# Up product of a hybrid encoder block: twelve of its tiles regrouped from pairs into threes, and the weight forms of every pair split 1024 columns at a time

## The chip, the cores and the metric

One core of one Trainium2 chip runs the whole kernel. The metric is the device time of one execution in microseconds (us), shown as the median of several runs. The profile and its trace are of one execution of the same program; times in it count from the start of its span.

## The reference

One layer of an encoder trunk over x of 512 tokens by 1024 features, all in float32:

```python
h  = rmsnorm(x, g_pre_mix)
q, k, v, g, u, sv, a_ret, a_sgu = split(h @ w_in)
merged = sigmoid(a_ret) * retention(q, k, v, g) @ w_ret_o + sigmoid(a_sgu) * sgu(u, sv) @ w_sgu_o
x  = x + rmsnorm(merged @ w_out, g_post_mix)
h2 = rmsnorm(x, g_pre_ffn)
hid = conv3(h2 @ w_up) + conv_b          # 1024 -> 2 * 2816, width-3 convolution over the tokens, per channel
a, b = split(hid)
x  = x + rmsnorm((gelu(a) * b) @ w_down, g_post_ffn)
```

The change is about `h2 @ w_up` (the up product) and about the way in which the weights of some products are made ready.

## The kernel before, in words

**Precision.** Every float32 operand of a matmul is split into a high part, which TensorE's fp32r format holds, and the rest: ScalarE copies the operand into the high tile, and VectorE subtracts that from the operand (`split`, lines 117 to 119). A product of two such operands is three matmuls, high by high, high by low and low by high (`mm3`, lines 299 to 302).

**Weights.** All weights come as tiles of 128 by 1024 from one array `wall`. A list of units, `units` (lines 126 to 159), gives the order in which they are used. `w_get` hands out the next unit and, ahead of use, has further units loaded and split so long as they fit in a look-ahead of nine slots; the slots (`w4`, nine of 128 by 1088) hold the finished high and low tiles, and four raw tiles (`raw`) hold what a DMA of SyncE's queue brings. A block unit (`w_block`) takes two slots: one for a high tile of 1024 columns, one for the low one.

**Blocks and pairs.** The up product makes 22 tiles of the hidden layer. A tile has two output blocks of 128 channels by 512 tokens, one for `a` and one for `b`. There are two ways to make a tile. Plain: two calls of `f_block`, each 8 x 3 matmuls with 512 moving columns, into one PSUM bank. In seven products (class `Pair`): the two blocks together by a Strassen-Winograd scheme, seven products of 4 x 3 matmuls with 256 moving columns, into three PSUM banks, with sums and differences of the activations made once beforehand (`h2_forms`). The products are spread over `part1` (four), `part2` (one) and `part3` (two). `part1` copies the first product out of its bank before the fourth adds to the same bank, `part2` reads bank 2 before `part3` adds to it, and the results end in two SBUF tiles `c` from a pool of six (`tmp`).

**Forms.** A pair needs seven weight operands of 512 columns: B11, B21, T1 to T4 and B22, where T1 to T4 are sums of the four quarters of the raw weights. In the kernel before, each is a unit of its own (`w_form`, lines 194 to 215), with one copy on ScalarE and one subtraction on VectorE of 512 columns, and one slot that holds the high and the low part. The four sums are additions of 512 columns on VectorE; for the gate weights two of them (T2, T4) are on GpSimd. Pairs are also used for the u product (4 pairs) and for the two gates (8 pairs), whose order is the hand-written list `MIDDLE`.

**Order in the up product.** Tiles 0 to 3 are plain. Tiles 4 to 19 go in couples (`COUPLES`): one tile as a pair, one plain. A couple runs `part1`, the first block of the plain tile, `part2`, half of the second block, `part3`, and the other half. Tiles 20 and 21 are plain. After its products each tile goes through `tile_done` (line 1309): for each of its blocks a scaled copy on ScalarE and two multiply-adds on VectorE (`conv`), then a gelu on ScalarE and a product on VectorE (`gated`). After certain tiles (7, 9, 11, 13, 17, and 19 to 21) `down_forms` prepares activations for the down product: four additions and one split on VectorE, more work on ScalarE and GpSimd's DMAs. The down product follows, with weight units "q" and "t" (`w_down`) that need three additions and two splits for each step.

**Order of the engines.** Instructions are traced in program order, and a planner in the framework puts them on each engine's queue by priority, readiness and its own estimate of costs; tiles of a pool are handed out as earlier ones come free. An engine then runs its queue in the order that was fixed.

Of the kernel before, what the change touches and what calls it, by code (L numbers as in the profile page):

```python
# [13 lines left out]
ALU = mybir.AluOpType  # L14

P = 128
# [27 lines left out]
COUPLES = [(i, i + 1) for i in range(4, 20, 2)]  # L44
# [8 lines left out]
def tile_block(ctx: ExitStack, tc, xT, x, wall, par, cs, wsp, bsp, gpost, gffn, out):  # L53
# [71 lines left out]
    FORMS = ("B11", "B21", "T1", "T2", "T3", "T4", "B22")  # L125
    units = []
    i = 0
    while i < NW:
# [6 lines left out]
        elif i == U0:  # L135
            us, gs = ([[(f, k + n * m) for f in FORMS] for n in range(KD // 2)] for k, m in ((U0, 2), (GATE0, 4)))
            ws = [("blk", GATE0 + 4 * (n // 2) + 2 + n % 2) for n in range(KD)]
            for what, n in MIDDLE:
                units += {"W": lambda: ws[n : n + 1], "U1": lambda: us[n][:4], "U2": lambda: us[n][4:],
                          "G1": lambda: gs[n][:4], "G2": lambda: gs[n][4:]}.get(what, list)()  # L140
            i = GATE0 + 2 * KD
        elif GATE0 <= i < GATE1:
            units += pair[:4] + [("blk", i + 2)] + pair[4:] + [("blk", i + 3)]
            i += 4
        elif i == UP0 + 2 * COUPLES[0][0]:
            for a, b in COUPLES:
                pair = [(f, UP0 + 2 * a) for f in FORMS]
                units += pair[:4] + [("blk", UP0 + 2 * b)] + pair[4:] + [("blk", UP0 + 2 * b + 1)]
            i = UP0 + 2 * COUPLES[-1][1] + 2
# [44 lines left out]
    def w_form(form, i):  # L194

        if form == "B11":
            a, b = raw_tile(), raw_tile()
            nc.sync.dma_start(a, wall[i])
            nc.sync.dma_start(b, wall[i + 1])
            w_raw["B11"], w_raw["B12"] = a[:, :S], a[:, S:]  # L200
            w_raw["B22"], w_raw["B21"] = b[:, :S], b[:, S:]
        elif form == "T1":
            t = raw_tile()
            w_raw["T1"], w_raw["T2"], w_raw["T3"], w_raw["T4"] = t[:, :S], t[:, S:], w_raw["B12"], t[:, S:]
            nc.vector.tensor_add(w_raw["T1"], w_raw["B11"], w_raw["B12"])
            nc.vector.tensor_add(w_raw["T3"], w_raw["B12"], w_raw["B22"])
            eng = nc.vector if i < GATE0 or i >= UP0 else nc.gpsimd
            eng.tensor_tensor(out=w_raw["T2"], in0=w_raw["T1"], in1=w_raw["B22"], op=ALU.add)
        elif form == "T4":
            eng = nc.vector if i < GATE0 or i >= UP0 else nc.gpsimd  # L210
            eng.tensor_tensor(out=w_raw["T4"], in0=w_raw["T2"], in1=w_raw["B21"], op=ALU.add)
        w = slot("wf", 0, 1088)
        lo, hi = w[:, AT_64 : AT_64 + S], w[:, S + AT_192 : 2 * S + AT_192]
        split(hi, lo, w_raw[form])
        return hi, lo
# [65 lines left out]
    def w_size(u):  # L281
        return 2 if u[0] in ("blk", "q", "t") or u[0][0] == "s" else 1
# [626 lines left out]
    class Pair:  # L909
# [9 lines left out]
        def product(self, b, act, first, w=None):  # L919
            wh, wl = w or w_get()  # L920
# [21 lines left out]
        def part1(self):  # L942
# [3 lines left out]
            def second():  # L946
                o = self.product(1, self.x(4, T0), True)
                self.sum = v.tensor_add(two(c0[:, T0]), o, two(c0[:, T0])).ins

            o = self.product(0, self.x(0, T0), True)  # L950
            copy(two(c0[:, T0]), o)
            second()
            self.product(2, self.s("S1"), True)
            o = self.product(0, self.s("S2"), False)
# [4 lines left out]
        def part2(self):  # L959
            c0, c1 = self.t  # L960
            o = self.product(0, self.s("S3"), False)
            copy(two(c1[:, T1]), o)
            v.tensor_sub(two(c1[:, T1]), self.two(self.b[2][:, T0]), two(c1[:, T1]))
            self.w = w_get(), w_get()
# [344 lines left out]
    def tile_done(i, o):  # L1309
        gated(*(conv(t, 2 * i + s_) for s_, t in enumerate(o)))  # L1310
        if i < COUPLES[-1][1]:
# [18 lines left out]
    couples = dict(COUPLES)  # L1330
    i = 0
    while i < NF:
        if i in couples:
            p = Pair(None, lambda: tmp("c"), (h2h, h2l, h2forms))
            p.part1()
            o = [f_block(h2h, h2l, KD)]
            p.part2()
            o.append(f_block(h2h, h2l, KD, p.part3))
            tile_done(i, p.t)
            tile_done(i + 1, o)  # L1340
            i += 2
# [237 lines left out]
def _two(a):  # L1579
# [3 lines left out]
        np.concatenate([b[:, 0, :, 0], b[:, 1, :, 0]], -1), np.concatenate([b[:, 1, :, 1], b[:, 0, :, 1]], -1),  # L1583
# [3 lines left out]
def _up(a):  # L1587

    for i, _ in COUPLES:
# [89 lines left out]
```

## Time and profile before

| what | value |
|---|---|
| median of 3 runs | 783.18 us (782.7 to 783.85) |
| span of the profiled execution | 782.6 us (no other time is given for it) |
| busy TensorE / weight load / VectorE / ScalarE / GpSimd | 774.5 / 720.7 / 639.5 / 485.2 / 103.5 us |
| granted TensorE clock, mean | 0.997 |
| matmul records | 5139 |
| HBM read / written | 91.34 MB / 4.19 MB |

Busy time is the union of an engine's instructions. Matmuls and VectorE's instructions overlap their neighbours at the ends, so the time that one more of them costs is read from start to start, not from its own length. In the text PE is TensorE, PEld its weight load, DVE VectorE, ACT ScalarE, POOL GpSimd and SP SyncE; L926 is line 926 of the kernel before.

### The profile page before, as it was taken

To read this page: it belongs to the slowest core of one execution; us is meant where nothing else is said; L and a number is where in the kernel's file an instruction comes from. 1 tells how busy PE (TensorE), PEld (TensorE's weight loads), DVE (VectorE), ACT (ScalarE), POOL (GpSimd) and SP (SyncE) were. 2 spreads that over 40 slices of the span, in tenths; PEclk is the share of its full clock that TensorE was granted. 3 is DMA by queue.
4 is the path that set the end of the run, shared out by engine and by line. 5 is a ranking of instruction groups with operands and counts; after the bars stand their busy time and mean duration, and the time that the engine had idled before them with its cause. 6 is when DMAs were issued, how large, how long until landed. Compare 5 with 4: busy or idle time off the path is not lost.

```text
span 782.6 us, 13472 instructions
## 1 busy us (share of the span) xinstructions
PE 774.5 (99%) x5139; PEld 720.7 (92%) x5139; DVE 639.5 (82%) x1093; ACT 485.2 (62%) x878; POOL 103.5 (13%) x132
## 2 busy tenths in 40 slices
PE   9999999999999999999999999999999999999996
PEld 8888998998999999999998998999999998999996
DVE  6567987789789988877765679989999889886987
ACT  7555568688466766644454686657777568644542
POOL 0040001130021102033211200001111012200001
PEclk9999999999999999999999999999999999999998
DMA  8783224453223233233459120435555375733344
GB/s 288 271 246 102 81 82 162 108 122 108 81 91 126 82 122 121 83 110 106 138 171 337 54 81 28 124 107 141 142 148 149 108 199 111 171 114 107 109 162 162
DMA packets 35889, 104.80 MB, mean 134 GB/s; under 512 B 4400, under 2 KB 6320, under 8 KB 35824
## 3 DMA queue, kind: packets, MB, share of 16 engines
q1 hardware_dynamic: 27936, 87.81, 34.0%
q0 software_dynamic: 7024, 14.95, 9.0%
q10 hardware_dynamic: 864, 1.18, 0.4%
q8 instruction: 40, 0.66, 0.4%
q14 instruction: 25, 0.20, 0.1%
HBM read 91.34 MB, written 4.19 MB: 122 GB/s over the span
## 4 chain that ended last, share of the span: by engine, by line
PE 92%; DVE 3%; DMA 3%; issue 1%; ACT 0%; POOLq 0%; DVEq 0%; POOL 0%; ACTq 0%
PE ps L926 24%; PE ps L300 12%; PE ps L302 12%; PE ps L301 12%; PE ps L1372 7%; PE ps L755 5%; PE ps L634 4%; PE ps L636 4%; PE ps L635 4%; DMA raw<-wall 3%; PE ps L1109 2%; PE ps L1108 2%; PE ps L1107 2%; DVE dl L119 1%; PE ps L997 1%
## 5 line engine op out<-in xcount | busy, mean ns | idle before, releaser
L119 DVE TENSOR_TENSOR wl<-raw,wh 128x1024 fp32r<-128x1024 f32 (+1 forms) x84 | 96.0, 1152 | 54.3 <-issue 19.1
L100 ACT ACTIVATE wf<-raw 128x512 fp32r<-128x512 f32 x140 | 85.6, 625 | 67.3 <-PE ps L301 19.4
L926 PE MATMUL ps<-sh,wf 128*128 128x256 f32 x640 | 117.4, 276 | 0.1
L119 DVE TENSOR_TENSOR wf<-raw,wf 128x512 fp32r<-128x512 f32 x140 | 107.0, 774 | 9.2 <-ACT wf L100 8.6
L926 PEld LDWEIGHTS ps<-sh,wf 128*128 128x128 f32 x640 | 101.9, 192 | 1.1 <-ACT sig L100 0.5
L100 ACT ACTIVATE wh<-raw 128x1024 fp32r<-128x1024 f32 (+2 forms) x88 | 84.8, 977 | 28.5 <-DMA raw<-wall 14.0
L300 PE MATMUL ps<-h2h,wh 128*128 128x512 f32 (+1 forms) x256 | 90.6, 354 | 0.0
L301 PE MATMUL ps<-h2l,wh 128*128 128x512 f32 (+1 forms) x256 | 90.4, 353 | 0.0
L302 PE MATMUL ps<-h2h,wl 128*128 128x512 f32 (+1 forms) x256 | 90.4, 353 | 0.0
L926 PE MATMUL ps<-sl,wf 128*128 128x256 f32 x320 | 88.0, 275 | 0.0
L926 PEld LDWEIGHTS ps<-sl,wf 128*128 128x128 f32 x320 | 61.4, 192 | 0.4
L1372 PE MATMUL ps<-dh,fh 128*128 128x256 f32 x216 | 59.6, 276 | 0.3 <-DVE yy L1409 0.3
L1372 PE MATMUL ps<-dl,fh 128*128 128x256 f32 x216 | 59.5, 275 | 0.0
L1372 PE MATMUL ps<-dh,fl 128*128 128x256 f32 x216 | 59.4, 275 | 0.0
L100 ACT ACTIVATE dh<-raw 128x768 fp32r<-128x768 f32 (+1 forms) x36 | 33.6, 950 | 33.8 <-DVE raw L231 15.2
L302 PEld LDWEIGHTS ps<-h2h,wl 128*128 128x128 f32 x256 | 48.6, 190 | 5.1
L301 PEld LDWEIGHTS ps<-h2l,wh 128*128 128x128 f32 x256 | 48.6, 190 | 4.5
L300 PEld LDWEIGHTS ps<-h2h,wh 128*128 128x128 f32 x256 | 48.6, 190 | 4.5
L926 PE MATMUL ps<-xh,wf 128*128 128x256 f32 x288 | 52.2, 275 | 0.0
L636 PE MATMUL ps<-wh,xl 128*128 128x512 f32 x128 | 48.5, 379 | 0.0
L635 PE MATMUL ps<-wl,xh 128*128 128x512 f32 x128 | 48.5, 379 | 0.0
L634 PE MATMUL ps<-wh,xh 128*128 128x512 f32 x128 | 48.5, 380 | 0.0
(343 smaller groups left out, 2171.6 us busy)
## 6 DMA issues: line engine op xcount, KB each, us to landing
raw<-wall SPq DMA_DIRECT2D x144, 512.0 KB, 3.7
x<-x SPq DMA_DIRECT2D x24, 256.0 KB, 6.0
fl<-gp POOLq DMA_DIRECT2D x12, 256.0 KB, 3.8
swap<-qkraw POOLq DMA_DIRECT2D x16, 128.0 KB, 4.8
x<-x POOLq DMA_DIRECT2D x8, 256.0 KB, 2.3
fl<-fs POOLq DMA_DIRECT2D x8, 256.0 KB, 4.3
xT<-xT SPq DMA_DIRECT2D x7, 256.0 KB, 5.0
xT<-xT POOLq DMA_DIRECT2D x4, 256.0 KB, 4.1
```

Source lines behind the costliest of these rows:

```text
L100: return nc.scalar.activation(out=o, in_=i, func=AF.Copy)
L119: low[0] = nc.vector.tensor_sub(lo, src, as32(hi)).ins
L300: nc.tensor.matmul(o, ah, bh, start=start, stop=False, skip_group_check=skip)
L301: nc.tensor.matmul(o, ah, bl, start=False, stop=False, skip_group_check=skip)
L302: pe_last[0] = nc.tensor.matmul(o, al, bh, start=False, stop=stop, skip_group_check=skip).ins
L634: nc.tensor.matmul(acc[t], xh[k][:, c], turns(wh[:, f]), start=k == 0, stop=False)
L635: nc.tensor.matmul(acc[t], xh[k][:, c], turns(wl[:, f]), start=False, stop=False)
L636: part_end[0] = nc.tensor.matmul(acc[t], xl[k][:, c], turns(wh[:, f]), start=False, stop=k == KD - 1)
L755: nc.tensor.matmul(bank[t], a_[:, c], turns(w_[:, f]), start=first and k == i == 0, stop=last and k == 3 and i == 2, skip_group_check=True,)
L926: self.last = nc.tensor.matmul(o, w_[:, c], a_, start=first and k == n == 0, stop=k == 3 and n == 2, skip_group_check=True,)
L1107: nc.tensor.matmul(o, ah, turns(bh), start=k == 0, stop=False)
L1372: nc.tensor.matmul(o, a_[:, c], turns(w_[:, f]), start=j == t == i == 0, stop=j == DP - 1 and i == 2 and n not in (M2, M3, M4), skip_group ...
```

## The change

`COUPLES` becomes `GROUPS`: (4, 5) and (6, 7) stay couples, and tiles 8 to 19 go in four groups of three, (8, 9, 10) to (17, 18, 19). In a three the first and the last tile go in seven products and the middle one is plain, so that ten tiles are made in seven products where there were eight. A three runs: `part1` of the first tile, the first half of a block of the middle tile, `part2`, the other half of that block, `part3`, `tile_done` of the first tile; then the same with the last tile and the middle tile's second block, with `tile_done` of the middle tile ahead of the last `part3`.

The seven forms become four units: B1 (B11 and B21 in one raw tile), T12 and T34 of 1024 columns and two slots each, and B22 of 512 columns and one slot. A copy and a subtraction of 1024 columns take the place of two of 512. The sums are the same four additions; T34 is now written over the raw tile of B1. This holds for all pairs, those of the u product and of the gates too. The host's layout of the raw weights changes to suit.

```diff
-COUPLES = [(i, i + 1) for i in range(4, 20, 2)]
+GROUPS = [(4, 5), (6, 7)] + [(i, i + 1, i + 2) for i in range(8, 20, 3)]
...
-    FORMS = ("B11", "B21", "T1", "T2", "T3", "T4", "B22")
+    FORMS = ("B1", "T12", "T34", "B22")
...
+            for a, b, *c in GROUPS:
                 pair = [(f, UP0 + 2 * a) for f in FORMS]
+                b = [("blk", UP0 + 2 * b + n) for n in range(2)]
+                if c:
+                    last = [(f, UP0 + 2 * c[0]) for f in FORMS]
+                    units += pair[:2] + b[:1] + pair[2:] + last[:2] + b[1:] + last[2:]
+                else:
+                    units += pair[:2] + b[:1] + pair[2:] + b[1:]
...
+        eng = nc.vector if i < GATE0 or i >= UP0 else nc.gpsimd
+        if form == "B1":
+            a, b = w_raw["a"], w_raw["b"] = raw_tile(), raw_tile()
             nc.sync.dma_start(a, wall[i])
             nc.sync.dma_start(b, wall[i + 1])
+            w_raw["B22"], w_raw["B12"] = b[:, :S], b[:, S:]
+            raw = a
+        elif form == "T12":
+            raw = w_raw["t"] = raw_tile()
+            nc.vector.tensor_add(raw[:, :S], w_raw["a"][:, :S], w_raw["B12"])
+            eng.tensor_tensor(out=raw[:, S:], in0=raw[:, :S], in1=w_raw["B22"], op=ALU.add)
+        elif form == "T34":
+            raw = w_raw["a"]
+            nc.vector.tensor_add(raw[:, :S], w_raw["B12"], w_raw["B22"])
+            eng.tensor_tensor(out=raw[:, S:], in0=w_raw["t"][:, S:], in1=raw[:, S:], op=ALU.add)
+        if form == "B22":
+            w = slot("wf", 0, 1088)
+            lo, hi = w[:, AT_64 : AT_64 + S], w[:, S + AT_192 : 2 * S + AT_192]
+            raw = w_raw["B22"]
+        else:
+            hi, lo = slot("wf", AT_192), slot("wf", AT_64)
+        split(hi, lo, raw)
...
-        return 2 if u[0] in ("blk", "q", "t") or u[0][0] == "s" else 1
+        return 1 if u[0] == "B22" else 2
...
+                o = [f_block(h2h, h2l, KD, p.part2)]
+                p.part3()
+                tile_done(i, p.t)
+                p = Pair(None, lambda: tmp("c"), (h2h, h2l, h2forms))
+                p.part1()
+                o.append(f_block(h2h, h2l, KD, p.part2))
+                tile_done(i + 1, o)
+                p.part3()
+                tile_done(i + 2, p.t)
```

`Pair` takes its operands through a new method `halves`, which gets one unit of 1024 columns and hands out its two halves.

84 lines of the change are left out of this document (35 added, 49 removed).

## The prediction

> **What bounds the kernel now.** I read the page's busy times and the shares of its chain first.
>
> ```profile
> span 782.6 us, 13472 instructions
> PE 774.5 (99%) x5139; PEld 720.7 (92%) x5139; DVE 639.5 (82%) x1093; ACT 485.2 (62%) x878; POOL 103.5 (13%) x132
> PE 92%; DVE 3%; DMA 3%; issue 1%; ACT 0%; POOLq 0%; DVEq 0%; POOL 0%; ACTq 0%
> ```
>
> TensorE holds 92% of the chain, so a matmul less is a gain only while the others keep up. Whether they do is read from the stages: two windows of the middle part, the eight couples of the up product, the last two plain tiles, and the entry into the down product (columns: PE, PEld, DVE, ACT, POOL, clock, DMA share, GB/s).
>
> ```profile
> 210.00:320.00 110.00, 110.00 (x849) 105.95 (x848) 96.91 (x163) 73.11 (x125) 17.88 (x13) 1.00 0.32 101
> 320.00:401.00 81.00, 80.91 (x554) 75.68 (x553) 63.65 (x94) 41.10 (x69) 17.71 (x12) 1.00 0.42 137
> ...
> 490.28:510.02 19.74, 19.74 (x135) 18.45 (x134) 19.11 (x31) 13.52 (x25) 1.83 (x2) 1.00 0.50 146
> 510.02:529.76 19.74, 19.74 (x135) 18.45 (x134) 16.89 (x27) 11.18 (x20) 0.00 (x0) 1.00 0.35 107
> 529.76:549.50 19.74, 19.74 (x135) 18.45 (x134) 18.16 (x31) 14.22 (x28) 3.50 (x4) 1.00 0.54 140
> 549.50:569.24 19.74, 19.74 (x135) 18.45 (x134) 18.15 (x31) 14.18 (x28) 3.50 (x4) 1.00 0.53 141
> 569.24:588.98 19.74, 19.74 (x135) 18.45 (x134) 18.48 (x32) 14.71 (x27) 2.59 (x3) 1.00 0.56 147
> 588.98:608.72 19.74, 19.74 (x135) 18.45 (x134) 18.49 (x32) 14.72 (x27) 2.56 (x3) 1.00 0.58 147
> 608.72:628.46 19.74, 19.74 (x135) 18.45 (x134) 16.90 (x27) 11.29 (x20) 0.00 (x0) 1.00 0.32 108
> 628.46:648.20 19.74, 19.74 (x134) 18.45 (x133) 16.26 (x29) 13.58 (x25) 3.03 (x4) 1.00 0.66 175
> 648.20:668.76 20.56, 20.56 (x98) 17.98 (x96) 19.47 (x35) 16.40 (x26) 4.65 (x6) 1.00 0.61 128
> 668.76:685.00 16.24, 16.24 (x146) 16.16 (x144) 14.56 (x24) 11.88 (x19) 3.71 (x5) 1.00 0.68 175
> ```
>
> Each couple takes the same 19.74 us and PE is full. But DVE is busy for 16.3 to 19.1 us of them: in this stage it is a second bound just behind the first. ACT (at most 14.72) and the DMAs (share at most 0.66) are not.
>
> **The matmuls.** The chain of waits in order of time gives their pace in one couple (start, length).
>
> ```profile
> 490.28 5.36 PE ps L926 x48
> 495.64 0.22 PE ps L300
> ...
> 500.82 1.34 PE ps L926 x12
> 502.16 0.22 PE ps L300
> ...
> 504.75 2.68 PE ps L926 x24
> ...
> 510.02 5.36 PE ps L926 x48
> ...
> 540.30 1.34 PE ps L926 x12
> ```
>
> A product of 12 matmuls of 256 columns takes 1.34 us (5.36 / 48 = 0.1117 each); a block of 24 matmuls of 512 columns goes from 495.64 to 500.82, 5.18 us. A tile in seven products takes 5.36 + 1.34 + 2.68 = 9.38 us, a plain one 2 x 5.18 = 10.36, so one more tile in seven products saves 0.98, and two save 1.96 us. The Trainium skill, page TensorE: Matmul & The Clock Gate, section Back-to-back issue gap, gives an isolated matmul on a warm clock N / 2.4 + 2.5 ns and says that this under-counts where N is small. By it the gap for 256 columns would be 109.2 ns, the pair 9.17 us and the saving an estimated 2.4 us instead of 1.96; the trace has 111.7 ns, so the measurement decides for 1.96.
>
> **VectorE's work.** Its timeline gives costs from start to start.
>
> ```profile
> 528.13 0.68 DVE L119 TENSOR_TENSOR wf<-raw,wf 128x512 fp32r<-128x512 f32 x1
> ...
> 630.12 0.75 DVE L1254 SCALAR_TENSOR_TENSOR cv<-c,part,cv 128x511 f32<-128x511 f32 x1
> 630.78 0.74 DVE L1254 SCALAR_TENSOR_TENSOR cv<-ps,part,cv 128x511 f32<-128x511 f32 x1
> 631.44 0.68 DVE L1263 TENSOR_TENSOR gp<-cv,cv 128x512 f32<-128x512 f32 x1
> 632.04 0.74 DVE L1250 SCALAR_TENSOR_TENSOR cv<-ps,part,cv 128x511 f32<-128x511 f32 x1
> ...
> 635.22 0.42 DVE L1289 TENSOR_TENSOR fs<-gp,gp 128x256 f32<-128x256 f32 x1
> 635.56 1.22 DVE L119 TENSOR_TENSOR wl<-raw,wh 128x1024 fp32r<-128x1024 f32 x1
> 636.69 0.42 DVE L1290 TENSOR_TENSOR fs<-fs,gp 128x256 f32<-128x256 f32 x1
> ```
>
> A multiply-add costs 0.66, an operation of 512 columns 0.60, of 1024 1.13, of 256 0.34 us. A pair's tile before: seven subtractions 4.20, four sums 2.40, three evacuations of 256 columns 1.02, four multiply-adds 2.64, the gating 0.60, together 10.86. With the merged forms the subtractions are 3 x 1.13 + 0.60 = 3.99 and the tile 10.65, a saving of 0.21. A plain tile is 2.26 + 2.64 + 0.60 = 5.50. The sum for a couple before, 16.36, stands against 16.89 busy in the couple that has no `down_forms`, a factor of 1.03; `down_forms` adds 1.3 to 1.6 (18.16 and 18.49 less 16.9), say 1.4.
>
> A three costs DVE (2 x 10.65 + 5.50) x 1.03 = 27.6 us, and PE 2 x 9.38 + 10.36 = 29.12. With `down_forms` after tiles 9; 11 and 13; none; and 17, the four threes need 29.0, 30.4, 27.6 and 29.0 of 29.12: 116.0 for PE's 116.5. DVE's spare time, 1 to 3 us in each couple before, is gone. The first three also inherits the evacuation of both tiles of couple (6, 7), 6.5 us where a three leaves about 4.5, so a backlog of 2.0 + 1.3 = 3.3 us builds up by the end of tiles 11 to 13.
>
> What covers it: weights are ready long ahead. The T3 form whose subtraction starts at 528.13 is used at 540.30, so weights may be 10 us late. What does not wait as long is the emptying of PSUM banks. The rows of one `part2`, from the chain and from the timelines of ACT and DVE:
>
> ```profile
> 560.04 1.34 PE ps L926 x12
> ...
> 562.25 0.37 ACT L100 ACTIVATE c<-ps 128x256 f32<-128x256 f32 x1
> ...
> 562.99 0.42 DVE L963 TENSOR_TENSOR c<-ps,c 128x256 f32<-128x256 f32 x1
> ...
> 565.40 1.23 DVE L119 TENSOR_TENSOR wl<-raw,wh 128x1024 fp32r<-128x1024 f32 x1 [1.40 <-issue]
> ...
> 569.54 0.75 DVE L1250 SCALAR_TENSOR_TENSOR cv<-ps,part,cv 128x511 f32<-128x511 f32 x1
> ```
>
> The subtraction that empties bank 2 ends at 563.33; S4's product needs the bank at 560.04 + 1.34 + 2.59 + 1.34 = 565.31, 2.0 us later. In a three `part2` comes half a block (2.59 us) earlier, while one tile less (3.24 us) is evacuated ahead of it, which leaves 2.6 us against a backlog of up to 3.3. Two smaller deadlines join it: the next `part1` writes a `c` tile that the last tile's or the middle tile's evacuation must have freed, and ACT's copies of banks stand in its queue behind a T12 that now waits for both of its sums. PE's waits in the threes thus lie between 0 (the planner puts evacuations first) and 3.3 us (the whole backlog). I take 1.0, nearer to the excess of 0.7 than to the whole.
>
> **The entry into the down product.** Here the lead is gone already before:
>
> ```profile
> 683.77 1.22 DVE L119 TENSOR_TENSOR dl<-raw,dh 128x1024 fp32r<-128x1024 f32 x1
> 684.92 0.68 DVE L226 TENSOR_TENSOR raw<-raw 128x512 f32<-128x512 f32 x1
> ...
> 684.84 0.28 PE L1372 MATMUL ps<-dh,fh 128*128 128x256 f32 x1
> 685.05 0.38 PE L1372 MATMUL ps<-dl,fh 128*128 128x256 f32 x1
> ```
>
> The split ends at about 684.92; PE's two starts stand 0.21 apart where 0.11 is its pace, so PE waits 0.1 us for it. If PE comes 1.96 us earlier, DVE must too. The cost lies between 0 (DVE's chain hangs on PE's end of tile 19 and moves along) and 1.96 (DVE comes no earlier). The last couple's 16.26 shows 3.5 us of idle DVE, since the weights that follow are four plain blocks, and most of the backlog can go there; I take 0.4.
>
> **Other parts, at nothing.** The 12 pairs of the middle stages save DVE 0.21 us each; PE was full there (110.00 of 110, 80.91 of 81), so no gain. Their T12 waits for GpSimd's T2 before either half can be split:
>
> ```profile
> L208 POOL TENSOR_TENSOR raw<-raw,raw 128x512 f32<-128x512 f32 x8 | 13.3, 1660 | 90.6 <-DMA raw<-wall 74.2 <-DVE raw L205 16.4
> ```
>
> 1.66 us, covered by a lead like the 10 us above; without cover, two sums in each of eight pairs would cost 26 us. DMAs: a three loads eight raw tiles of 0.52 MB in 29.12 us, 144 GB/s, where a couple loads five in 19.74, 133 GB/s; rows of 175 GB/s stand beside a full PE. The new turn of the raw tiles lets the next B1 load only after T34's split, still some 10 us ahead of use. Coarser units leave the slots the same: pair and block fill nine, as before.
>
> **Sum.** -1.96 + 1.0 + 0.4 = -0.56 us. The profiled span of 782.6 is 0.6 below the median of 783.18, and I apply the difference to the median: 782.6 us. What this measurement can tell from no change is about 0.2%, 1.57 us, so this forecast is no change.
>
> **Rivals.** *PE stays fed* (0.33): the planner lets evacuations pass, DVE's chain into the down product moves along, and the waits stay under 0.38 us: 783.18 - 1.96 = 781.2. For it: no PE gap in eight couples at up to 19.11 us of DVE. Against: 116.0 of 116.5. *VectorE's queue becomes the bound* (0.24), the other side: at 565.40 DVE idles 1.40 us for a slot while a finished bank, read only at 569.54, could have been worked on. Where such idling stays in the threes, there is no slack to take it. Half of 1.40 in each of the eight halves is 5.6 us: 783.18 - 1.96 + 5.6 = 786.8; it decides from 0.44 us a half, 3.5 in all. The Trainium skill, same page, section on the array's architecture (16x 32x32), says that ACT's and DVE's queues are strict FIFO; by that rule no ready work passes a waiting head, and the trace's 1.40 us agrees.
>
> **Chances.** No change 0.43 (waits from 0.38 to 3.5 us), faster 0.33, slower 0.24. The range, 781.0 to 786.0, reaches from the fed case to the middle of the slower one and leaves out about 0.2; the likeliest case alone is 781.6 to 784.7.
>
> **What would show it.** Right: 72 more matmuls, threes of 29.1 us in the chain plus 0.1 to 0.5 each in front of an S2, S4 or T4 product, released by ACT or DVE; DVE over 28 us busy in the threes with tiles 9, 11, 13 and 17; a PE gap at the third or fourth step of the down product. Wrong: PE gaps at `wf` tiles (weights late), gaps in the gates' stage behind POOL, or DVE with several us to spare in the threes.

## The result: 0.7% slower

The changed kernel takes 788.70 us (median of 6, 788.00 to 791.97) against 783.23 us (median of 6, 782.70 to 783.85): a ratio of 1.0072 (95% interval 1.0059 to 1.0086), 5.5 us slower where 0.6 us faster was forecast.

The spans must be brought to one footing first. Wherever a run of these two kernels is listed with its span, the run takes 1.7 to 1.9 us longer (788.33 for the profiled 786.6 here; 783.32 for 781.6 of the kernel before, in a later comparison). By that, an estimate, the profiled execution of before, with its span of 782.6, was one of about 784.4, above the six runs counted here (single later runs go beyond it). This is most of the reason why the spans differ by 4.0 us and the medians by 5.5. It also means that the stage lengths of before, below, are together about 1 us too long, and it is not known in which stage.

The page of the changed kernel (span, busy time by engine):

```profile
span 786.6 us, 13545 instructions
PE 773.9 (98%) x5211; PEld 721.9 (92%) x5211; DVE 642.7 (82%) x1051; ACT 482.9 (61%) x830; POOL 105.6 (13%) x132
```

There are 72 matmuls more, as the change intends, and PE is busy 0.6 us less in a span that is 4.0 us longer: PE waits. The windows by stage say where. Before the change (middle part from the first product of a pair, w_out with the transposes and plain tiles, up product from the first couple, down product; columns as in the prediction):

```profile
210.20:403.02 192.82, 192.73 (x1409) 183.21 (x1408) 162.53 (x258) 114.73 (x194) 36.87 (x26) 1.00 0.36 115
403.02:490.12 87.10, 87.10 (x514) 79.28 (x512) 63.24 (x120) 56.53 (x140) 11.34 (x19) 1.00 0.34 122
490.12:668.76 178.64, 178.64 (x1154) 165.76 (x1152) 162.06 (x268) 123.85 (x218) 21.66 (x25) 1.00 0.52 138
668.76:782.55 113.79, 106.62 (x949) 106.05 (x947) 92.37 (x159) 51.64 (x88) 6.34 (x9) 0.98 0.43 137
```

and the same four stages after it:

```profile
209.72:405.04 195.32, 193.23 (x1410) 183.65 (x1409) 159.89 (x225) 109.08 (x160) 38.90 (x26) 1.00 0.35 111
405.04:492.13 87.09, 87.09 (x513) 79.39 (x512) 63.24 (x117) 57.00 (x139) 11.34 (x19) 1.00 0.35 122
492.13:673.05 180.92, 178.26 (x1226) 166.67 (x1225) 169.35 (x264) 124.89 (x205) 19.97 (x23) 1.00 0.50 133
673.05:786.55 113.50, 106.36 (x949) 105.98 (x947) 91.62 (x160) 53.09 (x91) 8.05 (x11) 0.99 0.48 142
```

The middle part is 2.5 us longer (195.32 less 192.82), though no matmul was added there. The up product is 2.28 us longer, though it has 1.96 us less for PE to do. The other two stages are within 0.3 us of before. PE's waits (who waited <- for whom: total, times, longest), after:

```profile
PE ps L938 <- ACT c L100: 2.6, 4, 1.2
PE ps L938 <- ACT u L100: 1.9, 2, 1.3
PE ps L410 <- PEq L1692: 0.8, 1, 0.8
PE ps L1398 <- DVE yy L1435: 0.3, 1, 0.3
PE ps L938 <- ACT sig L100: 0.2, 1, 0.2
```

The rows for PEq and `yy` stand in the answer for before too, and nothing else does. The three others are new, and all are of one kind: a product (L938) waits until ACT has copied a bank out of PSUM, `c` in the up product, `u` and `sig` in the middle part. No row names a weight. From start to start of the matmuls, the excess over PE's pace adds up to 2.7 us in the middle part (four places, 235 to 262 us) and 3.6 us in the up product (six places, 496 to 626 us; all but 0.3 us, at 496 us in couple (4, 5), in the threes). The question is why ACT, busy 61% of the time, copies late.

ACT's timeline at the first of these places, in the middle part:

```profile
227.16 1.06 ACT L100 ACTIVATE wf<-raw 128x1024 fp32r<-128x1024 f32 x1 [1.16 <-DVE sig L960]
228.13 0.36 ACT L100 ACTIVATE sig<-ps 128x256 f32<-128x256 f32 x1
231.79 1.09 ACT L100 ACTIVATE wh<-raw 128x1024 fp32r<-128x1024 f32 x1 [3.30 <-DMA raw<-wall]
232.76 0.63 ACT L1067 ACTIVATE u<-u 128x512 f32<-128x512 f32 x1
...
234.78 0.63 ACT L1067 ACTIVATE u<-u 128x512 f32<-128x512 f32 x1 [1.11 <-DVE u L993]
235.31 0.36 ACT L100 ACTIVATE u<-ps 128x256 f32<-128x256 f32 x1
```

and PE's row there:

```profile
235.73 0.38 PE L938 MATMUL ps<-sh,wf 128*128 128x256 f32 x1 [0.56 <-ACT u L100]
```

ACT stands idle for 3.30 us in front of a weight block whose load has not landed. The delay reaches `u`'s bank copy through two queues: VectorE is idle 0.89 us for the block's copy, the scaling of `u` (L993) runs behind the block's subtraction at 234.06, ACT waits 1.11 us for that scaling, and the bank copy comes behind it. PE waits for that copy, not for the weights: the block itself is first used at 239.85 us. The load itself was issued late. The load of the same block in SyncE's timeline, after and then before:

```profile
228.25 0.33 SPq L181 DMA_DIRECT2D raw<-wall  x1
```

```profile
225.53 0.33 SPq L176 DMA_DIRECT2D raw<-wall  x1
```

2.7 us later. SyncE's queue held it for a VectorE subtraction (L119), 6.4 us after the change and 2.6 us before:

```profile
SPq L181 <- DVE wf L119: 6.4, 1, 6.4
```

```profile
SPq L176 <- DVE wf L119: 2.6, 1, 2.6
```

Before the change the same copy had no idle time in front of it:

```profile
229.26 1.05 ACT L100 ACTIVATE wh<-raw 128x1024 fp32r<-128x1024 f32 x1
```

Ahead of the longest of the four places, 1.5 us at 262 us, ACT stands in front of a block once more:

```profile
259.60 1.06 ACT L100 ACTIVATE wh<-raw 128x1024 fp32r<-128x1024 f32 x1 [2.86 <-DMA raw<-wall]
```

These two places make 2.2 of the 2.7 us; between them, ahead of the two small ones, no block is late.

In the up product the head of the queue is another one. ACT before T4's first product of the first three:

```profile
541.31 0.63 ACT L100 ACTIVATE fh<-fs 128x512 fp32r<-128x512 f32 x1 [3.38 <-DVE fs L1305]
...
542.51 0.71 ACT L100 ACTIVATE fh<-gp 128x256 fp32r<-128x256 f32 x2
...
543.73 0.71 ACT L1287 ACTIVATE fl<-fh 128x256 fp32r<-128x256 f32 x2
544.35 1.04 ACT L100 ACTIVATE wf<-raw 128x1024 fp32r<-128x1024 f32 x1
545.29 0.36 ACT L100 ACTIVATE c<-ps 128x256 f32<-128x256 f32 x1
```

ACT is idle 3.38 us in front of the first copy of `down_forms`, for a sum on VectorE. Then the other copies of `down_forms` and a merged weight copy run, and only then the bank copy that PE waits for until 545.71. What ACT itself waited for in the four threes says the same (531.88 to 652.32; what waits, for whom, total, times, longest):

```profile
ACT wf L100 <- DVE raw L211: 9.5, 4, 3.7
ACT fh L100 <- DVE fs L1305: 7.8, 4, 3.4
ACT cv L1276 <- DVE cv L1269: 4.1, 4, 2.1
ACT c L100 <- PE ps L938: 2.9, 3, 1.7
```

In the six couples before (529.76 to 648.20) it read:

```profile
ACT c L100 <- PE ps L926: 17.2, 12, 2.6
ACT fh L100 <- DVE fs L1290: 11.7, 6, 3.0
```

A bank copy that waits 17.2 us for PE is ahead of PE. That lead has shrunk to 2.9 us. The wait for `fs` is not new; the one of 9.5 us was 0.4 us before, and the one of 4.1 us is not in the answer for before. In these, too, ACT waits for VectorE. VectorE has nearly no idle time left, three by three:

```profile
531.88:562.04 30.16, 29.38 (x217) 27.89 (x216) 28.71 (x44) 20.36 (x36) 3.51 (x4) 1.00 0.45 122
562.04:592.26 30.22, 29.65 (x218) 27.69 (x217) 29.55 (x48) 23.75 (x43) 6.09 (x7) 1.00 0.55 131
592.26:621.62 29.36, 29.36 (x218) 27.93 (x217) 27.87 (x44) 20.10 (x34) 2.56 (x3) 1.00 0.59 157
621.62:652.32 30.70, 29.50 (x219) 28.04 (x218) 28.34 (x44) 22.09 (x36) 2.56 (x3) 1.00 0.47 140
```

### The profile page after: what moved, and what is told of

It reads as the page before. It is cut to its first block, busy times and chain, and to the rows that moved or that the text cites. A ratio compares the mean times of both kernels' runs of the same rounds, so it can differ in the third digit from the quotient of the medians.

```text
span 786.6 us, 13545 instructions
## 1 busy us (share of the span) xinstructions
PE 773.9 (98%) x5211; PEld 721.9 (92%) x5211; DVE 642.7 (82%) x1051; ACT 482.9 (61%) x830; POOL 105.6 (13%) x132
## 5 line engine op out<-in xcount | busy, mean ns | idle before, releaser
L938 PE MATMUL ps<-sh,wf 128*128 128x256 f32 x704 | 130.5, 277 | 3.7 <-ACT u L100 1.9
L119 DVE TENSOR_TENSOR wl<-raw,wh 128x1024 fp32r<-128x1024 f32 (+1 forms) x80 | 90.5, 1141 | 43.2 <-ACT wh L100 22.8
L938 PEld LDWEIGHTS ps<-sh,wf 128*128 128x128 f32 x704 | 112.5, 192 | 5.7 <-ACT c L100 2.5
L100 ACT ACTIVATE wf<-raw 128x1024 fp32r<-128x1024 f32 x88 | 82.8, 947 | 53.6 <-DVE raw L211 18.6
L119 DVE TENSOR_TENSOR wf<-raw,wf 128x1024 fp32r<-128x1024 f32 x88 | 103.8, 1181 | 13.0 <-ACT wf L100 11.4
L938 PE MATMUL ps<-sl,wf 128*128 128x256 f32 x352 | 97.0, 275 | 0.0
L308 PE MATMUL ps<-h2h,wh 128*128 128x512 f32 (+1 forms) x224 | 78.6, 351 | 0.0
L309 PE MATMUL ps<-h2l,wh 128*128 128x512 f32 (+1 forms) x224 | 78.4, 350 | 0.0
L310 PE MATMUL ps<-h2h,wl 128*128 128x512 f32 (+1 forms) x224 | 78.4, 350 | 0.0
L938 PEld LDWEIGHTS ps<-sl,wf 128*128 128x128 f32 x352 | 67.6, 192 | 0.4
L938 PE MATMUL ps<-xh,wf 128*128 128x256 f32 x288 | 52.2, 276 | 0.0
L310 PEld LDWEIGHTS ps<-h2h,wl 128*128 128x128 f32 x224 | 42.6, 190 | 4.2
```

Source lines behind the costliest of these rows:

```text
L100: return nc.scalar.activation(out=o, in_=i, func=AF.Copy)
L119: low[0] = nc.vector.tensor_sub(lo, src, as32(hi)).ins
L308: nc.tensor.matmul(o, ah, bh, start=start, stop=False, skip_group_check=skip)
L309: nc.tensor.matmul(o, ah, bl, start=False, stop=False, skip_group_check=skip)
L310: pe_last[0] = nc.tensor.matmul(o, al, bh, start=False, stop=stop, skip_group_check=skip).ins
L938: self.last = nc.tensor.matmul(o, w_[:, c], a_, start=first and k == n == 0, stop=k == 3 and n == 2, skip_group_check=True,)
```

## The experiments

Two theories at the start. A: the merged forms do the harm, because one copy must wait for two sums and blocks ACT's queue. B: the threes do it, because they ask too much of VectorE and ACT. Each time below is a median, with the ratio to the kernel before (783.5 to 783.8 us, timed beside them) and its 95% interval.

### The parts of the change by themselves

Threes with the seven old forms; couples with the merged forms; threes with merged forms in the up product alone. The edits are the two settings

```diff
-GROUPS = [(4, 5), (6, 7)] + [(i, i + 1, i + 2) for i in range(8, 20, 3)]
+GROUPS = [(i, i + 1) for i in range(4, 20, 2)]          # couples
-    FORMS = ("B1", "T12", "T34", "B22")
+    FORMS = ("B11", "B21", "T1", "T2", "T3", "T4", "B22")  # in u and gates, or in all
```

with the old branches of `w_form` and the old layout of the raw weights where the old forms are used.

> Threes as in the change, but all pairs keep the seven separate 512-column forms. Theory A (the merged 1024-column forms are what hurts: one copy of 1024 columns has to wait for two sums, and the bank copies stand behind it in ACT's queue): the 2.7 us of PE waits in the middle part go back to about 0, and of the 3.6 us in the threes at most 1 is left; with 1.96 us of PE work saved the time is 781 to 782.5 us. Theory B (the threes themselves ask too much of VectorE and ACT, whatever the forms): the middle part recovers its 2.5 us, the waits in the threes stay at 3 us or more, and the time is 784.5 to 786.5 us.

> Couples as before the change, with merged forms in all pairs. Theory A: the middle part loses the same 2.5 us as in the changed kernel, and PE waits appear in the couples too, 1 to 3 us before S2, S3 or S4 products released by ACT's copies; time 786.5 to 788.5 us. Theory B: the middle part loses 2.5 us but the couples stay free of waits over 0.1 us; time about 785.7 us.

> Threes with merged forms in the up product, the seven 512-column forms in the middle part (u and both gates). If the trace's gaps are read rightly, the 2.7 us of PE waits in the middle part vanish and nothing else moves: 785.7 to 786.4 us, by theory A and theory B alike. If the middle part's slowness had another cause (the weights' start, another phase of the queues), the time stays near 788.7 us.

| | middle part, us | up product, us | time, us | ratio |
|---|---|---|---|---|
| before | 192.82 | 178.64 | 783.67 | |
| threes, old forms | 192.92 | 183.02 | 787.55 | 1.0051 (1.0037 to 1.0065) |
| couples, merged in all | 195.82 | 179.54 | 788.81 | 1.0066 (1.0054 to 1.0079) |
| threes, merged in the up product | 193.11 | 180.69 | 785.66 | 1.0025 (1.0016 to 1.0035) |
| the change: threes, merged in all | 195.32 | 180.92 | 788.70 | 1.0072 (1.0059 to 1.0086) |

The times of the first two lie above the ranges of both theories, and each theory holds in one stage and fails in the other. Merging costs 2.2 to 3.0 us in the middle part, with threes or without. The threes alone cost 3.9 us (787.55 less 783.67), and beside them merging *helps* in the up product, by 1.9 us (787.55 to 785.66), the opposite of theory A. In couples it does not help: with merged forms the up product is 0.9 us longer than before, though PE waits for no bank copy there. PE's wait for bank copies in the up product, with old forms and then with merged ones, shows it:

```profile
PE ps L957 <- ACT c L100: 4.0, 5, 1.4
```

```profile
PE ps L957 <- ACT c L100: 2.3, 4, 1.1
```

Merging takes 3.6 us of work from VectorE there (172.90 to 169.29 us busy in this stage); that this is why it helps was not tested by itself. So, by the medians, the change is +3.9 (threes), -1.9 (merged forms beside them) and +3.0 (merged forms in the middle part).

### The middle part: what merging does

Five edits, all on the kernel before (couples, old forms in the up product) with merged forms in the middle part: the sums T2 and T4 on VectorE; only B1 merged; T34 written into T12's raw tile; the look-ahead at ten half slots; the plain blocks not loaded.

```diff
-        eng = nc.vector if i < GATE0 or i >= UP0 else nc.gpsimd
+        eng = nc.vector                                         # sums on VectorE
-    FORMS = ("B1", "T12", "T34", "B22")
+    FORMS = ("B1", "T1", "T2", "T3", "T4", "B22")               # only B1 merged
...
-            raw = w_raw["a"]
+            raw = w_raw["t"]                                    # T34 in T12's tile
...
-            eng.tensor_tensor(out=raw[:, S:], in0=w_raw["t"][:, S:], in1=raw[:, S:], op=ALU.add)
+            eng.tensor_tensor(out=raw[:, S:], in0=raw[:, S:], in1=w_raw["a"][:, S:], op=ALU.add)
...
-... max(room, 9 if look == LOOK else 0)
+... max(room, 10 if look == LOOK else 0)                        # look-ahead
...
+        no_load = GATE0 <= i < GATE1                            # plain blocks of the middle part
...
-        if i > 1:
+        if i > 1 and not no_load:
             nc.sync.dma_start(raw, wall[i])
...
+            elif no_load:
+                with behind():
+                    for n, f in enumerate((slice(0, S), slice(S, 2 * S))):
+                        split(hi[:, f], lo[:, f], as32(xh[n]))
```

> Couples and separate forms in the up product as before the change; merged forms in the middle part only, and there T2 and T4 are summed on VectorE instead of GpSimd. Merging in the middle part cost 2.6 to 3.0 us (its length 195.3 to 195.8 us against 192.8 to 193.1). Theory P (T12's one copy waits at the head of ACT's queue for GpSimd's T2, and the bank copies wait behind it): the middle part goes back to 193 to 193.5 us and the time is 783.4 to 784.3 us. Theory R (the copies wait for loads, since a raw tile is held until T34 is split, and GpSimd is not the cause): the waits stay and the time is 786 to 787 us.

> Couples and separate forms in the up product as before the change; in the middle part only B11 and B21 go as one 1024-column form, T1 to T4 stay separate, T2 and T4 on GpSimd. Theory P: no copy waits for two sums any more, the middle part is 193 to 193.5 us long and the time 783.4 to 784.3 us. If coarser pieces as such (a 1024-column copy of 1.06 us where 0.63 was) make the bank copies late, about a third of the loss stays: 784.5 to 785 us.

> Couples and separate forms in the up product, merged forms in the middle part with T2 and T4 on GpSimd, but T3 and T4 are put into the raw tile of T1 and T2, so the tile of B11 and B21, the oldest of the four, is given back after T4's sum instead of after T34's split. Theory R (the next weight block's load waits for that tile, its copy stands idle at the head of ACT's queue, and bank copies wait behind it): the load that was issued at 228.1 us goes out 1 to 2.5 us earlier, the waits shrink to 1 us or less, the middle part is 193 to 194 us long and the time 783.4 to 784.7 us. If the coarser copies and the wait for two sums are the cause, whichever tile is held: 785.5 to 786.5 us, as with the sums on VectorE.

> Couples and separate forms in the up product, merged forms in the middle part; the look-ahead of the weights may reach over ten half slots instead of nine (the slots themselves stay nine). Theory L (a merged form of size 2 does not fit where one half slot is left, so loads are put into the queues one step later): the middle part goes from 195.5 to 193 to 194 us, 783.4 to 784.7 us. If the look-ahead is not the cause: 785.5 us or more.

> Couples and separate forms in the up product, merged forms in the middle part; the 16 plain weight blocks of the middle part are not loaded (two halves of x that lie in SBUF are split in their place, so these products are not the reference's). Theory R (their loads come late because raw tiles are given back later, their copies stand idle at the head of ACT's queue, and the bank copies behind them keep PE waiting): all waits over 0.4 us vanish, the middle part is 192.8 to 193.3 us and the time 783.2 to 784.2 us. If the merged copies' waits for two sums make the loss by themselves: 2 us or more of waits stay, 785.3 us or more.

| edit | middle part, us | time, us | ratio |
|---|---|---|---|
| sums on VectorE | 195.46 | 786.13 | 1.0033 (1.0021 to 1.0044) |
| only B1 merged | 194.28 | 784.63 | 1.0017 (1.0008 to 1.0026) |
| T34 in T12's tile | 198.43 | 788.84 | 1.0068 (1.0055 to 1.0082) |
| look-ahead of ten | 195.61 | 786.22 | 1.0031 (1.0021 to 1.0042) |
| plain blocks not loaded (work left out) | 192.49 | 783.69 | 0.9995 (0.9986 to 1.0004) |

GpSimd's sums are not the cause (theory P falls): without them the same four waits stand at the same places. Nor is the look-ahead. Only the last edit removes the loss, and it removes all of it. ACT's largest waits in the middle part of that run:

```profile
ACT mh L100 <- POOL sig L1117: 12.6, 7, 2.1
ACT wf L100 <- POOL raw L234: 10.0, 3, 4.5
```

The merged copies still wait 10.0 us for GpSimd's second sum, up to 4.5 us at a time, and PE waits for no other engine in this stage:

```profile
209.55:402.04 192.49, 192.49 (x1409) 183.38 (x1408) 162.23 (x238) 110.14 (x173) 36.59 (x26) 1.00 0.24 77
```

So theory R holds as far as this edit can show: the waits for two sums alone cost PE nothing, and the late loads of the plain blocks, standing at the head of ACT's queue, are what PE pays for when everything is merged. The edit also makes the ring of four raw tiles easier for the pairs' own loads, so the two cannot be told apart. The attempt to give the oldest raw tile back sooner went wrong: T3's sum then has to wait until T12 has been split out of that tile, the block's load goes out at 230.33 us instead of 228.25, and the middle part gets longer still, 198.43 us. A part of that is a lower clock: after a PE wait of 2.1 us, matmuls of 256 columns start 0.21 us apart from 239.0 to 242.3 us, twice the pace of 0.11 (granted clock 0.99 in this stage, 1.00 in the others). A fifth raw tile was not tried.

With only B1 merged the loss is about 1.1 us, and one wait of 1.3 us is left near 235 us. No block is late there, since its load goes out at 224.99 us. VectorE is idle 2.30 us for a load of the pair's own raw weights, in front of T1's sum, and ACT stands idle for that sum:

```profile
228.07 0.64 ACT L100 ACTIVATE wf<-raw 128x512 fp32r<-128x512 f32 x1 [2.46 <-DVE raw L221]
```

So a head of queue other than a late block may cost PE time too. Merging the sums accounts for the larger part of the loss, not for all of it.

### The threes: load, or order

All on the kernel with threes, merged forms in the up product and old forms in the middle part (785.66 us; 3.4 us of waits in the up product). First `down_forms` moved to tiles 4, 5, 6, 7 and 15, which was run on the whole change (788.70 us):

```diff
-            if i in (7, 9, 11, 13, 17):
+            if i in (4, 5, 6, 7, 15):
```

> The changed kernel with its down_forms calls at tiles 4, 5, 6, 7 and 15 instead of 7, 9, 11, 13 and 17: only one of them is left in the threes. If down_forms' copies, which stand ahead of a bank's copy in ACT's queue and wait there for VectorE, make the waits in the threes (part of theory B), about 2 of the 3.6 us go: 786 to 787 us, and VectorE's busy share of the first two threes falls by about 1.4 to 2.8 us. If only the merged forms matter (theory A), the waits stay: 788 to 789 us.

792.50 us (1.0113, 1.0100 to 1.0127), wrong by both theories. A buffer that was not in question decides: the one call left in the threes waits for a slot of `blk` that an accumulating DMA of an earlier call still reads.

```profile
647.84 0.42 ACT L100 ACTIVATE fa<-gp 128x256 fp32r<-128x256 f32 x1 [4.64 <-DMA fl<-gp]
```

PE waits 3.5 us for the bank copy behind it, and its clock then falls (granted 0.95 from 621 to 656 us; matmuls of 512 columns 0.43 us apart near 652 us, 0.22 before), so the wait costs more than its length. The run says nothing of load or order. Next, three ways to give VectorE less to do (T2 and T4 on GpSimd; the second multiply-add of the convolution on 1 column; B1's low half by an ACT copy and an accumulating DMA), and one to change the order (`down_forms` behind the next bank copy):

```diff
-        eng = nc.vector if i < GATE0 or i >= UP0 else nc.gpsimd
+        eng = nc.vector if i < GATE0 else nc.gpsimd             # sums on GpSimd
...
+        e = 1 if 16 <= m < 40 else S - 1                        # less for VectorE
-            out=c[:, 0 : S - 1], in0=o[:, 1:S], ...
+            out=c[:, 0:e], in0=o[:, 1 : e + 1], ...
...
+        if form == "B1" and i >= UP0 + 16:                      # low half by DMA
+            split_added(hi, lo, raw)
...
+            with tc.issue_after(ins):                           # order: ins is a bank copy
+                down_forms(len(dforms))
```

> Threes with merged forms in the up product, separate forms in the middle part (785.66 us), and T2 and T4 of the up product summed on GpSimd: VectorE has 1.2 us less to do in each pair's tile, 2.4 us in a three. Theory B (VectorE has no time to spare in the threes): the waits of 3.4 us shrink to 1 or less and the time is 782.5 to 783.5 us. If a T12 that waits for GpSimd blocks ACT's queue as in the middle part, new waits take their place: 786 us or more.

> Threes with merged forms in the up product, separate forms in the middle part (785.66 us), and in the tiles of the threes the second multiply-add of the convolution covers 1 column instead of 511, so this part of the computation is left out: VectorE has about 0.6 us less in each half, 3.5 us in a three, and nothing else changes. Theory B: the 3.4 us of waits in the up product vanish, 782 to 783 us. If ACT's own work or the order in which the pieces are queued makes the bank copies late, not VectorE's load, most of them stay: 784.5 us or more.

> Threes with merged forms in the up product, separate forms in the middle part (785.66 us), and in the eight pairs of the threes the low half of B1 is made by an ACT copy of minus the high half and an accumulating DMA, as the kernel does for down_forms, instead of by VectorE: VectorE has 1.13 us less in each pair's tile, 2.3 us in a three, ACT about 0.95 us more in each. Theory B: 783.2 to 784.2 us. If ACT's queue is as tight as VectorE's, its longer work eats the gain: 785.5 us or more.

> Threes with merged forms in the up product, separate forms in the middle part (785.66 us), and the down_forms after tiles 9, 11 and 17 are queued on each engine behind the next bank copy (ACT's), not ahead of it. If the place of down_forms' copies in ACT's queue makes the waits near 542, 568, 587 and 594 us (1.9 us together), 1.2 us or more of them goes: 783.8 to 784.5 us. If VectorE's load alone decides (theory B), the same waits appear at other copies: 785.2 to 786.2 us.

| edit | time, us | ratio |
|---|---|---|
| sums on GpSimd | 790.19 | 1.0083 (1.0069 to 1.0097) |
| less for VectorE (work left out) | 783.13 | 0.9997 (0.9989 to 1.0006) |
| B1's low half by DMA | 796.68 | 1.0164 (1.0150 to 1.0178) |
| `down_forms` behind | 785.98 | 1.0033 (1.0022 to 1.0045) |

Work that is left out brings 2.5 us. Work that is *handed to another engine* costs 4.5 and 11 us, although VectorE's load falls. With the sums on GpSimd, VectorE is busy 110.0 of the 122 us from 530 to 652, where it was 116.2, and ACT's first wait there is

```profile
ACT wf L100 <- POOL raw L229: 14.8, 6, 4.6
```

and with the DMA in the chain VectorE itself stands still, since T3's sum (L232) is written over the raw tile that the DMA still reads (530 to 660 us):

```profile
DVE raw L232 <- DMA wf<-raw: 15.5, 7, 5.2
```

A busy share does not say this: each hand-over puts a wait at the head of an in-order queue, and the reading of the banks is behind it. Other costs are in these times too. Beside the sums on GpSimd, VectorE's own T3 sum of 512 columns takes 0.94 us on average, 0.68 without them (ten each), and with the DMA the granted clock is 0.97 from 530 to 652 us, 1.00 without it. Queueing `down_forms` behind one bank copy only moves the waits to the next (0.72, 0.82 and 1.65 us near 568, 594 and 624, where they were 0.41, 0.14 and 1.25).

Four more runs, to divide the cost: both edits together with `down_forms` of tile 7 queued behind as well; two threes with couples between (the couples with the old forms); `down_forms` left out of the threes; and that with less for VectorE.

```diff
-GROUPS = [(4, 5), (6, 7)] + [(i, i + 1, i + 2) for i in range(8, 20, 3)]
+GROUPS = [(4, 5), (6, 7, 8), (9, 10), (11, 12), (13, 14, 15), (16, 17), (18, 19)]   # two threes
...
-            if i in (7, 9, 11, 13, 17):
-                down_forms(len(dforms))
+            if i in (9, 11, 13, 17):                             # left out of the threes
+                dforms.append(dforms[0])
+            elif i == 5:
+                down_forms(len(dforms))
```

> Threes with merged forms in the up product, separate forms in the middle part, the convolution's second multiply-add cut to 1 column in the threes (left out, as in the run with less work for VectorE, 783.13 us), and all down_forms of tiles 7, 9, 11 and 17 queued behind the next bank copy. If the two waits left there (0.95 us near 542 and 0.69 near 600) come from down_forms' copies ahead of a bank copy, they go: 781.3 to 782.1 us, the whole of the 1.96 us that PE saves. If VectorE or ACT is late for another reason, 1 us or more stays: 782.7 us or more.

> Middle part with separate forms; in the up product couples with separate forms and only two threes, with merged forms, each with couples around it: (4,5) (6,7,8) (9,10) (11,12) (13,14,15) (16,17) (18,19), nine tiles in seven products, 0.98 us of PE work saved. Theory B (a three leaves VectorE a backlog that the next couple's 1 to 3 us of spare time can take): waits of 0.5 us or less, 782.6 to 783.3 us, faster than before the change by up to 0.1%. If a three costs what it does by its own order of banks, backlog or not (E3's 3.4 us over four threes is 0.85 each): 784 to 785 us.

> Threes with merged forms in the up product, separate forms in the middle part (785.66 us); down_forms runs after tile 5 instead of 7, and after tiles 9, 11, 13 and 17 it is left out (the forms of the first pair of tiles are used again in their place). If down_forms' chain in the queues makes most of the 3.4 us of waits, at most 1.2 us stays: 783.5 us or less. If VectorE's load and its in-order hand-overs with ACT make them without it, 2 us or more stays: 784.3 us or more. In between, both have a share.

> As the run without down_forms in the threes, and with the convolution's second multiply-add cut to 1 column in the threes (both left out). If these two are all that keeps the bank copies late, the waits in the threes are 0.4 us or less and PE's saving of 1.96 us shows whole: 781.5 to 782.3 us. If a part of the order itself (part2 half a block earlier) is late whatever the load, 1 us or more stays: 782.7 us or more.

| edit | time, us | ratio |
|---|---|---|
| less for VectorE (work left out), `down_forms` behind | 786.45 | 1.0034 (1.0021 to 1.0046) |
| two threes among couples | 785.25 (782.84 to 787.55) | 1.0014 (1.0003 to 1.0026) |
| no `down_forms` in the threes (work left out) | 782.92 | 0.9989 (0.9980 to 0.9998) |
| that, and less for VectorE (work left out) | 781.34 | 0.9976 (0.9965 to 0.9987) |

The last row gives PE's saving whole: 2.35 us below before, of which 1.96 is the saving, and the list of PE's waits names no bank copy. From 785.66 us the two omissions bring 2.5 and 2.7 us alone and 4.3 together, so the two overlap, and together they carry the cost; the threes' order of `part2` is not late by itself. VectorE's load is not the whole of it: the first omission takes 10.0 us off its busy time in the up product (169.29 to 159.30), the second only 4.6 (to 164.65), for about the same gain. But leaving `down_forms` out takes VectorE's work, ACT's copies (10.3 us of ACT's busy time) and the waits between them away at once, so their shares cannot be told apart. Reordering is no substitute: with `down_forms` queued behind, the gelu that waits for the late convolution stands in front of the bank copy, whose product waits 1.5 us.

```profile
550.54 0.63 ACT L1297 ACTIVATE cv<-cv 128x512 f32<-128x512 f32 x1 [0.96 <-DVE cv L1290]
551.08 0.36 ACT L100 ACTIVATE c<-ps 128x256 f32<-128x256 f32 x1
```

The two threes among couples have 0.98 us less for PE and runs from 782.84 to 787.55 us, a spread of 4.7 us where the other three changed kernels timed beside it have 1.4 to 1.6 (the kernel before had 3.2 in its 25 runs there). The profiled one (783.17) has one wait of 1.0 us; what happens in the slow ones was not seen, and why they spread stays open.

Last, a complete kernel by that reading: `down_forms` after tiles 4, 5, 6, 7 and 13.

```diff
-            if i in (7, 9, 11, 13, 17):
+            if i in (4, 5, 6, 7, 13):
```

> Threes with merged forms in the up product, separate forms in the middle part, and down_forms after tiles 4, 5, 6, 7 and 13, so that one of five is left in the threes; nothing is left out. If it is down_forms in the threes that costs 2.4 us, wherever else it stands: about 1.0 us from VectorE's load and 0.5 us from the one that is left, 782.7 to 783.5 us, at or just below the kernel before. If four of them in two couples fill VectorE's queue there and the backlog is carried into the threes, or if the later one waits long for its buffers as in the earlier run with tile 15: 785 us or more.

788.79 us (1.0065, 1.0051 to 1.0079): the rival's case. PE waits 4.5 us for `c` copies, 2.5 of them at one place near 625 us, where a bank copy stands behind a merged weight copy and a gelu. So moving four of the five calls ahead of the threes does not give back what leaving them out gave; why this place is so late was not tested. No complete version here beats the kernel before.

## Why the prediction was wrong

*The matmuls, -1.96.* Right: 72 more, and a gain of 2.35 us shows where no bank copy holds PE (781.34 us). By the formula on the Trainium skill's page TensorE: Matmul & The Clock Gate, section Back-to-back issue gap, the saving would be an estimated 2.4 us. The times of the runs do not separate the two, since that run also leaves out other work; the rows' 111.7 ns decide for 1.96.

*Waits in the threes, 1.0 of a range of 0 to 3.3.* The term was mis-sized: the trace has 3.4 us in the threes (0.3 more in couple (4, 5)), at the upper end of the range, where 1.0 was put into the sum. By the medians it is some 0.5 us more: the run at 785.66 us is 3.95 above what PE's saving alone would leave (783.67 less 1.96), and its trace has 3.4 us of waits in the whole up product. VectorE's demand was forecast well (116.0 of 116.5; it was busy 114.5 of 120.4). What failed is the reading of the range as a backlog of VectorE that the planner drains by putting evacuations first. PE waited for ACT, in front of S2, S3 and T4 products, and ACT's copies were held by a head of queue that waited for VectorE: the prediction had this as one of "two smaller deadlines" behind a T12 that waits for both sums. That T12 waits 9.5 us is so, yet beside the threes merging as a whole saves 1.9 us. `down_forms`, which the prediction priced as VectorE's 1.4 us alone, also stands in ACT's queue ahead of bank copies; left out of the threes, it gives back 2.7 us.

*Entry into the down product, +0.4.* Wrong, and harmless: no wait at its third or fourth step; the stage is 0.3 us shorter than before.

*DMAs, at nothing.* The count was wrong, and harmless: four threes load 24 raw tiles, six each and not eight, and a couple loads four and not five. Nothing in the up product waited long for a load (ACT 2.0 us in all in the threes).

*Middle part, "at nothing".* This is the step that failed outright: +2.5 us in the trace, 3.0 in the medians. The working covered T12's wait with a lead of 10 us of ready weights, and the new turn of the raw tiles with "still some 10 us ahead of use". Both hold for the weights (the late block was used first at 239.85 us, 11.6 us after its load went out), and no product waited for a weight. The copy, however, does not wait alone: it holds ACT's queue, and a bank copy behind it has little lead: before the change ACT was 0.4 us early for a `sig` bank of the middle part (it waited 3.6 us for PE over nine of them) and 1.4 us for a `c` bank of the couples (17.2 over twelve). The load of a plain block that slips by 2.7 us is hidden from PE as a weight and still costs PE 0.7 us as a block at the head of ACT's queue. The gaps came behind ACT, not behind GpSimd as the list of signs had it. With separate forms in the middle part the threes take 785.66 us, inside the range of 781.0 to 786.0; with merged ones, 788.70.

*The rivals.* "VectorE's queue becomes the bound" put 5.6 us of waits in the threes, from a wait on VectorE; 3.4 came, by this kind of mechanism and at its deciding point of 3.5 us, but through ACT's queue and with the other share of the loss in a stage that no rival named. Its 1.40 us did not show what it was read for: the bank read at 569.54 had first to be copied by ACT, at 568.46, so VectorE had no work of that bank to pass over. Its 786.8 and the range's 786.0 were both too low for want of the middle part's loss. The rule the prediction cited beside it, strict FIFO, is also in the Trainium skill's page Perfetto Trace Analysis, section Per-instruction lifecycle: what the profiler-reported window actually captures. The run with `down_forms` after tile 15 agrees: ACT stayed idle until 647.84 us in front of one copy, although PE, out of work from about 646.0, was waiting for a bank copy behind it. Applied to ACT in the middle part, the rule would have pointed to a loss.

## What to carry to other kernels

A cover belongs to one consumer: "the weights are 10 us early" hides a late weight from PE, but the copy that makes it stands in an in-order queue, and the lead that counts is that of the work queued behind it, here bank copies that were 0.4 to 1.4 us ahead on average. Before merging or delaying an operation, look up what is behind it on its engine in the timeline, and price the wait by that. When a second engine is nearly as full as the first, leave work out before moving it: both hand-overs in the up product, to GpSimd and to a DMA, made this kernel slower, though VectorE had less to do.

## What the runs showed of the hardware

VectorE's subtraction of 1024 columns, both inputs in SBUF, took 1.22 us as a rule, and 1.97 and 2.23 us beside a sum on GpSimd (VectorE, then GpSimd, in the changed kernel):

```profile
241.36 1.97 DVE L119 TENSOR_TENSOR wf<-raw,wf 128x1024 fp32r<-128x1024 f32 x1
...
243.59 2.23 DVE L119 TENSOR_TENSOR wf<-raw,wf 128x1024 fp32r<-128x1024 f32 x1
```

```profile
240.65 1.60 POOL L211 TENSOR_TENSOR raw<-raw,raw 128x512 f32<-128x512 f32 x1 [20.67 <-DVE raw L210]
243.46 1.28 POOL L215 TENSOR_TENSOR raw<-raw,raw 128x512 f32<-128x512 f32 x1 [1.21 <-DVE wf L119]
```

The page SBUF — State Buffer of the Trainium skill, section SBUF: two separate sides, says that GpSimd and a VectorE operation with two SBUF inputs exclude each other for a whole instruction. By that rule the first subtraction would run from the sum's end at 242.25 and finish at 243.47, the second from 244.74 to 245.96; by the rows they finish at 243.33 and 245.82, so the rows agree to 0.14 us. This does not carry the loss of the middle part: with those sums on VectorE it was as long (195.46 us).
